# The last normalisation with its scale worked out on transposed statistics, and eight of its tiles prepared by TensorE

## The chip, the cores and the metric

One core of one Trainium2 chip runs the whole kernel in one launch. The metric is the device time of that launch in microseconds (us): 2783.64 as the median of three runs (2782.03 to 2784.01). Below, PE is TensorE, ACT is ScalarE, DVE is VectorE, POOL is GpSimd and SP is the engine that issues most DMAs.

## The reference

Two layers of a streaming encoder work on 288 tokens (256 of a prompt and 32 of a running stream) of width 2048. Layer 0 mixes tokens by a gated MLP, layer 1 by retention; each is followed by a SwiGLU network. After every one of these four parts comes the same step:

```python
def layer_norm(x, g, b):
    mu = jnp.mean(xf, axis=-1, keepdims=True)
    var = jnp.mean(jnp.square(xf - mu), axis=-1, keepdims=True)
    y = (xf - mu) * lax.rsqrt(var + LN_EPS) * g + b
...
x = layer_norm(ALPHA * x + swiglu(x, w_ffn_in[i], w_ffn_out[i]), ln_ffn_g[i], ln_ffn_b[i])
```

The case is about the last of these four normalisations, whose result is the output `yT`.

## The kernel before, in words

All activations lie transposed: 128 features on the partitions and the 288 tokens along the free axis, so that the width of 2048 makes 16 tiles of 128x288, kept in `y`. Weights stream from memory in chunks of 128x1024 fp32. SP loads a chunk into a `raw` buffer (three of them rotate), ACT casts it into a high part (L435) and DVE subtracts that into a low part (L436); PE then makes three products of each 128x128 block (L106 to L108). A chunk is prepared three chunks ahead of its use.

The output product of the last SwiGLU finishes one of the 16 output tiles after another, and `PostNorm.last` is called as each is done. It adds the tile to `y` (L236), subtracts a coarse centre (L284), squares on ACT (L286) and adds tile and square into two running sums (L289, L290). With the last but one tile it also writes an identity and a row of minus ones into a `raw` buffer named `centring` (L254 to L257). After the last tile, `stats` sums over the partitions by matmuls with a constant matrix, which leaves mean `m1` and mean square `m2` of every token, the same on all 128 partitions, in two PSUM banks (L302, L305).

`finish` then normalises. It writes the order of DVE, ACT and POOL out by hand (`manual_schedule` with the three engines of `FINISH`); PE is in hand-written order throughout, and SP takes its DMAs in the order in which they are issued in the code. Its parts:

- The scale `ap` = 1/sqrt(variance) is worked out on full 128x288 tiles: square of the mean and variance (L355, L362), logarithm and exponential on ACT (L363, L364), and one Newton step on DVE (L366 to L368). Variance and scale lie in PSUM; a copy `a` of the scale in SBUF is made for POOL (L370).
- Tiles are handled in pairs (L334, 128x576). Centring subtracts the mean, scaling multiplies by the scale. POOL does both for the pairs 4, 8 and 10, with copies of mean and scale in SBUF. DVE does the pairs 0, 2 and 14, with mean and scale in PSUM. For tiles 6, 7, 12 and 13 PE makes the centred tile in PSUM (L358, L359), and DVE multiplies it by `a` (L341).
- Gain and bias are then applied tile by tile, by ACT for eleven tiles (L351) and by DVE for five (L349), and each finished pair is stored (L352). The first pair stored is 0 and the last store is tile 13; one single tile goes through ACT's queue.

PSUM has eight banks, four in the rotating pool `acc` and four in `aux`.

Of the kernel before, what the change touches and what calls it, by code (L numbers as in the profile page):

```python
# [10 lines left out]
F32 = mybir.dt.float32  # L11
# [3 lines left out]
ALU = mybir.AluOpType  # L15
# [4 lines left out]
P = 128  # L20
# [17 lines left out]
GN_EPS = 1e-6  # L38
CB = 8
RAW = 3  # L40
NBLK = KT * 32 + KT * KT + KT * 96 + 32 * KT + 2 * (KT * 2 * HT + HT * KT)
NSTATE = HEADS * CB
NCH = (NBLK + NSTATE) // CB
# [148 lines left out]
class PostNorm:  # L192
# [38 lines left out]
    def last(self, m, ps, first_part=False):  # L231
        nc, lnp, gi = self.nc, self.lnp, self.gi
        if first_part:
            self.part(m, ps)
        else:
            nc.vector.tensor_tensor(self.y[:, m, :], ps[:, :NT], self.y[:, m, :], ALU.add)  # L236
        if self.n == 0:
            self.s = lnp.tile([P, 2, NT], F32, tag="sums", name=f"sums{gi}")
            nc.gpsimd.memset(self.s, 0.0)
            if self.out is not None:  # L240
                self.core.tables("natural_log_exp_and_others")
            else:
                if gi == 0:
                    self.core.tables("silu_and_others")
                gb = self.cst["ln"][:, gi, :, :].rearrange("p a k -> p k a")
                nc.scalar.copy(self.xh[:, :, NT:NX], gb)
                nc.vector.tensor_tensor(self.xl[:, :, NT:NX], gb, self.xh[:, :, NT:NX].bitcast(F32), ALU.subtract)
            r = self.tmp("cen", F32R)
            nc.scalar.copy(r, self.y[:, m, :])
            self.core.after(2, lambda: self.center(r))  # L250
        self.n += 1
        if self.out is not None and self.n == KT - 1:
            room = self.core.wp.tile([P, CB * P], F32, tag="raw", name="centring", bufs=3)
            self.ident, self.minus = room[:, :P], room[:, P:2 * P]  # L254
            make_identity(nc, self.ident)
            nc.gpsimd.memset(self.minus, 0.0)
            nc.gpsimd.memset(self.minus[:1, :], -1.0)  # L257
            d = self.y[:, KT - 1, :]
            nc.vector.tensor_tensor(d, d, self.c, ALU.subtract)
        if self.c is None:  # L260
            self.wait.append(m)
        else:
            self.sums(m)
        if self.n == (KT if self.out is None else KT - 1):
            self.parts = [[self.tmp(f"s{i}{j}", F32R) for j in range(2)] for i in range(2)]
            for i, (hi, lo) in enumerate(self.parts):
                split(nc, hi, lo, self.s[:, i, :])
        if self.n == KT:
            self.core.after(1 if self.out is not None else 2, lambda: self.stats(m))

    def center(self, r):

        nc = self.nc
        ps = self.core.bank(f"cen{self.gi}")
        nc.tensor.matmul(turned(ps[:, :NT]), self.cst["one_r"], turned(r), start=True, stop=True)
        self.c = self.lnp.tile([P, NT], F32, tag="cen", name=f"cens{self.gi}")
        nc.scalar.mul(self.c, ps[:, :NT], float(KT))
        for q in self.wait:
            self.sums(q)
# [16 lines left out]
    def stats(self, m):  # L296
# [18 lines left out]
        rsqrt(nc, a, v, t)  # L315
        nc.vector.scalar_tensor_tensor(b, m1, -1.0, a, ALU.mult, ALU.mult)

    def finish(self, m1, m2):


        nc, core, a, mean = self.nc, self.core, self.a, self.b
        mm = nc.tensor.matmul
        ap = core.bank("ap")[:, :NT]
        v = core.accum("fin")[:, :NT]
        t, r = self.tmp("t"), self.tmp("r")
        pool = (4, 8, 10)
        copied = (6, 7, 12, 13)
        late = (10, 11, 13, 14, 15)
        row = lambda k: self.y[:, k:k + 2, :]
        off = {k: (core.bank if i == 3 else core.accum)(f"off{k}")[:, :NT] for i, k in enumerate(copied)}  # L330

        def pair(k, op, vec, gp):
            eng, f = (nc.gpsimd, gp) if k in pool else (nc.vector, vec)
            eng.tensor_tensor(row(k), row(k), f.unsqueeze(1).broadcast_to([P, 2, NT]), op)  # L334

        center = lambda k: pair(k, ALU.subtract, m1, mean)

        def scale(k):
            if k in copied:
                for i in (k, k + 1):  # L340
                    nc.vector.tensor_tensor(self.y[:, i, :], off[i], a, ALU.mult)  # L341
            else:
                pair(k, ALU.mult, ap, a)

        def affine(k, n=2, queue=None):
            for i in range(k, k + n):
                d = self.y[:, i, :]
                if i in late:
                    nc.vector.tensor_scalar(d, d, self.gain(i), self.bias(i), ALU.mult, ALU.add)  # L349
                else:  # L350
                    nc.scalar.activation(d, d, AF.Identity, bias=self.bias(i), scale=self.gain(i))  # L351
            (queue or nc.sync).dma_start(self.out[:, k:k + n, :], self.y[:, k:k + n, :])  # L352

        with core.tc.manual_schedule(engines=FINISH):
            nc.scalar.activation(t, m1, AF.Square)  # L355
            nc.scalar.copy(mean, m1)
            for k in copied:
                mm(off[k], self.ident, self.y[:, k, :], start=True, stop=False)  # L358
                mm(off[k], self.minus, mean, start=False, stop=True)  # L359
            for k in pool:  # L360
                center(k)
            nc.vector.scalar_tensor_tensor(v, m2, LN_EPS, t, ALU.add, ALU.subtract)  # L362
            nc.scalar.activation(t, v, AF.Ln)  # L363
            nc.scalar.activation(r, t, AF.Exp, scale=-0.5)  # L364
            center(0)
            nc.vector.scalar_tensor_tensor(ap, v, -0.5, r, ALU.mult, ALU.mult)  # L366
            nc.vector.tensor_tensor(ap, ap, r, ALU.mult)
            nc.vector.scalar_tensor_tensor(ap, ap, 1.5, r, ALU.add, ALU.mult)  # L368
            scale(0)
            nc.scalar.copy(a, ap)  # L370
            for k in pool:
                scale(k)
            center(2)
            affine(0)
            scale(6)
            affine(6)
            scale(2)
            affine(4)
            affine(2)
            center(14)  # L380
            scale(12)
            affine(8)
            scale(14)
            affine(14)
            affine(10)
            affine(12, 1, nc.scalar)
            affine(13, 1)

    def norm(self, k):
        nc, d = self.nc, self.y[:, k:k + 2, :]  # L390
# [521 lines left out]
@with_exitstack  # L912
def hybrid_step(ctx, tc, ins, outs):
    nc = tc.nc
    ctx.enter_context(tc.manual_schedule(engines={PE}))
    core = Core(ctx, tc, ins["wpack"])
    cp = ctx.enter_context(tc.tile_pool(name="cp", bufs=1))
    lnp = ctx.enter_context(tc.tile_pool(name="lnp", bufs=1))
    cp.tile([P, 88], F32, name="shift")
    lnp.tile([P, 32], F32, name="shift_lnp")  # L920
    xh = moving(cp, KT, "xh")
    xl = moving(cp, KT, "xl")
    y = cp.tile([P, KT, NT], F32, name="y")
    cst = {}
    cp.tile([P, 40], F32, name="shift_one")
    cst["one2048"] = cp.tile([P, P], F32, name="one2048")
    nc.gpsimd.memset(cst["one2048"], 1.0 / D)
    cst["ln"] = cp.tile([P, 4, 2, KT], F32, name="lnv")
    cst["one_r"] = cp.tile([P, P], F32R, name="one_r")
    cp.tile([P, 56], F32, name="shift_end")  # L930
    core.tables("gelu_and_others")
    nc.scalar.copy(cst["one_r"], cst["one2048"])
    warm = core.bank("warm")
    for _ in range(11):
        nc.tensor.matmul(warm[:, :P], cst["one2048"], cst["one2048"], start=True, stop=True)

    def load(k):
        if k < KT:
            if k % 2 == 0:
                nc.sync.dma_start(y[:, k:k + 2, :], ins["xT"][:, k:k + 2, :])  # L940
            split(nc, xh[:, k, :NT], xl[:, k, :NT], y[:, k, :])

    with tc.manual_schedule(engines={mybir.EngineType.DVE, mybir.EngineType.Activation}):
        core.prep(0, lambda: load(0))
        for k in range(1, 4):
            load(k)
            core.prep(k)
    x = (xh, xl)
    ln = gmlp(core, cst, x, y, lnp, ins, outs["v"], lambda s: load(s + 4))
    ln = ffn(core, cst, x, y, lnp, 0, ln)  # L950
    ln = retention(core, cst, x, y, lnp, ln, ins, outs["st_p"], outs["st_s"])
    ffn(core, cst, x, y, lnp, 1, ln, outs["yT"])
    core.flush()
    assert len(core.order) == NBLK + NSTATE
    return core.order
# [84 lines left out]
```

## Time and profile before

| what | value |
|---|---|
| median of three runs | 2783.64 us (2782.03 to 2784.01) |
| the profiled execution's own time | 2784.02 us |
| its span in the profile | 2781.9 us |
| PE busy | 2769.4 us (100%) |
| DVE, ACT, POOL busy | 1695.2, 1239.0, 141.4 us (61%, 45%, 5%) |
| moved by DMA | 515.49 MB, mean 185 GB/s |
| last product of the last SwiGLU starts | 2764.83 us after the span's start |
| last store issued | 2777.49 us |
| bytes written by the stores of `yT` | 2.36 MB |

A share of busy time says which engine the whole span belongs to. The stretch that the change touches is the last 17 us; it has to be read from the timeline of that stretch, engine by engine, and from the transfers in it. An instruction's line in a timeline gives its start, its duration, engine, line, operation, output and inputs, and in brackets how long the engine was idle before it and what ended that; "x3" merges three in a row, and the duration is then that of all three.

### The profile page before, as it was taken

The numbers are of one execution on the slowest core, as the hardware profiler recorded it, in microseconds if no ns is written. First come the engines' busy times: TensorE is split into PE (matmuls) and PEld (weight loads), VectorE is DVE, ScalarE is ACT, GpSimd is POOL, SyncE is SP. The second block draws the span as 40 slices with busy tenths as digits, with TensorE's granted clock in tenths as the row PEclk, the third lists the DMA queues.
The fourth block names the chain that finished last, engine by engine and source line by source line (L and its number), as shares of the span: only waits on it lengthen the run. The fifth ranks groups of instructions, "written<-read, shape, count | busy, mean of one in ns | idle before, by whom it ended". The sixth has DMA issues, their size and how long they took to land.

```text
span 2781.9 us, 51416 instructions
## 1 busy us (share of the span) xinstructions
PE 2769.4 (100%) x21574; PEld 2755.9 (99%) x21574; DVE 1695.2 (61%) x2432; ACT 1239.0 (45%) x1641; POOL 141.4 (5%) x241
## 2 busy tenths in 40 slices
PE   9999999999999999999999999999999999999998
PEld 9999999999999999999999999999999999999998
DVE  6688964445444466877765666767864445444465
ACT  5455553333343344554543444445653433333343
POOL 1100000000000000012200111200000000000001
PEclk9999999999999999999999999999999999999999
DMA  8655555555555555567765666755555555555553
GB/s 281 214 186 167 171 169 174 174 174 174 175 173 172 176 177 175 178 199 244 232 197 173 198 216 217 230 193 173 167 175 174 174 172 173 173 174 175 174 174 125
DMA packets 146584, 515.49 MB, mean 185 GB/s; under 512 B 18016, under 2 KB 20336, under 8 KB 146320
## 3 DMA queue, kind: packets, MB, share of 16 engines
q1 hardware_dynamic: 131984, 473.47, 51.4%
q0 software_dynamic: 14224, 38.59, 4.6%
q8 instruction: 168, 2.75, 0.4%
q14 instruction: 64, 0.52, 0.1%
q10 hardware_dynamic: 144, 0.15, 0.0%
HBM read 486.98 MB, written 25.17 MB: 184 GB/s over the span
## 4 chain that ended last, share of the span: by engine, by line
PE 97%; DVE 1%; DMA 1%; issue 0%; POOL 0%; ACT 0%; DVEq 0%; POOLq 0%
PE af_in L107 13%; PE af_in L108 13%; PE af_in L106 13%; PE ab_in L107 7%; PE ab_in L106 7%; PE ab_in L108 7%; PE af_out L108 6%; PE af_out L107 6%; PE af_out L106 6%; PE ab_out L106 2%; PE ab_out L108 2%; PE ab_out L107 2%; PE aa_in L108 2%; PE aa_in L106 2%; PE aa_in L107 2%; PE aa_out L107 1%
## 5 line engine op out<-in xcount | busy, mean ns | idle before, releaser
L436 DVE TENSOR_TENSOR wlo<-raw,whi 128x1024 fp32r<-128x1024 f32 (+1 forms) x892 | 1085.5, 1218 | 865.4 <-ACT whi L435 859.8
L435 ACT CAST whi<-raw 128x1024 fp32r<-128x1024 f32 (+1 forms) x892 | 931.5, 1046 | 1374.4 <-issue 325.9
L107 PE MATMUL af_in<-xl,whi 128*128 128x288 f32 (+1 forms) x2816 | 814.3, 289 | 0.0
L108 PE MATMUL af_in<-xh,wlo 128*128 128x288 f32 (+1 forms) x2816 | 814.1, 289 | 0.0
L106 PE MATMUL af_in<-xh,whi 128*128 128x288 f32 (+1 forms) x2816 | 813.3, 289 | 0.0
L108 PEld LDWEIGHTS af_in<-xh,wlo 128*128 128x128 f32 x2816 | 527.8, 187 | 0.0
L107 PEld LDWEIGHTS af_in<-xl,whi 128*128 128x128 f32 x2816 | 527.8, 187 | 0.0
L106 PEld LDWEIGHTS af_in<-xh,whi 128*128 128x128 f32 x2816 | 527.7, 187 | 0.0
L107 PE MATMUL ab_in<-xl,whi 128*128 128x288 f32 (+1 forms) x1536 | 444.9, 290 | 0.3
L106 PE MATMUL ab_in<-xh,whi 128*128 128x288 f32 (+1 forms) x1536 | 444.3, 289 | 0.0
L108 PE MATMUL ab_in<-xh,wlo 128*128 128x288 f32 (+1 forms) x1536 | 443.7, 289 | 0.0
L107 PE MATMUL af_out<-hl,whi 128*128 128x288 f32 x1408 | 405.9, 288 | 0.0
L106 PE MATMUL af_out<-hh,whi 128*128 128x288 f32 x1408 | 405.9, 288 | 0.0
L108 PE MATMUL af_out<-hh,wlo 128*128 128x288 f32 x1408 | 405.9, 288 | 0.0
L107 PEld LDWEIGHTS ab_in<-xl,whi 128*128 128x128 f32 x1536 | 288.0, 187 | 1.9 <-DVE xl L436 0.7
L106 PEld LDWEIGHTS ab_in<-xh,whi 128*128 128x128 f32 x1536 | 287.9, 187 | 0.9
L108 PEld LDWEIGHTS ab_in<-xh,wlo 128*128 128x128 f32 x1536 | 287.9, 187 | 0.0
L106 PEld LDWEIGHTS af_out<-hh,whi 128*128 128x128 f32 x1408 | 263.8, 187 | 0.0
L107 PEld LDWEIGHTS af_out<-hl,whi 128*128 128x128 f32 x1408 | 263.8, 187 | 0.0
L108 PEld LDWEIGHTS af_out<-hh,wlo 128*128 128x128 f32 x1408 | 263.8, 187 | 0.0
L106 PE MATMUL aa_in<-xh,whi 128*128 128x288 f32 x512 | 148.5, 290 | 0.0
L108 PE MATMUL aa_in<-xh,wlo 128*128 128x288 f32 x512 | 147.8, 289 | 0.2 <-DVE wlo L436 0.2
(246 smaller groups left out, 2906.1 us busy)
## 6 DMA issues: line engine op xcount, KB each, us to landing
raw<-in_wpack_dram SPq DMA_DIRECT2D x887, 512.0 KB, 3.3
v_room<-tv POOLq DMA_DIRECT2D x32, 144.0 KB, 5.0
of<-o_room POOLq DMA_DIRECT2D x32, 144.0 KB, 4.5
vw<-v_room POOLq DMA_DIRECT2D x8, 512.0 KB, 5.7
out_st_s_dram<-sso POOLq DMA_DIRECT2D x16, 256.0 KB, 2.8
o_room<-to POOLq DMA_DIRECT2D x8, 512.0 KB, 3.9
out_st_p_dram<-so POOLq DMA_DIRECT2D x16, 256.0 KB, 5.8
y<-in_xT_dram SPq DMA_DIRECT2D x8, 288.0 KB, 5.4
```

What stands on the lines that cost most here:

```text
L106: mm(ps, hi, xh, start=first, stop=False)
L107: mm(ps, hi, xl, start=False, stop=False)
L108: mm(ps, lo, xh, start=False, stop=last)
L435: nc.scalar.copy(hi, f)
L436: nc.vector.tensor_tensor(lo, f, hi.bitcast(F32), ALU.subtract)
```

## The change

The statistics are transposed in blocks of 32x32, so that one column of nine blocks holds each of the 288 tokens once (32 partitions by 9 columns, repeated on the four quarters of the partitions). Variance, logarithm, exponential and Newton step work on these nine columns; two results are spread back to 288 columns by transposing a broadcast view: `a` = 1/sqrt(variance) and a row of sqrt(variance). `rows` has minus the mean in its first 32 partitions and the square root in the next 32.

For tiles 0 to 7 (`PRE`), PE makes gain * (y - mean) + bias * sqrt(variance) in PSUM: first a product with a diagonal matrix that carries the gain, then one with two rows, gain and bias, against `rows`. DVE multiplies that by `a` (`scaled`), and the pair is stored without further work. The pairs 8, 10 and 12 are centred by POOL and 14 by DVE; POOL scales 8 and 10, DVE scales 12 and 14; ACT applies gain and bias to these eight tiles. `a` and the mean's copy lie in SBUF; the nine-column work lies in SBUF.

The identity, the diagonal matrices and the two rows are made in `factors`, with the last but one tile, in three `raw` buffers instead of one. The two rows come from a new input by two DMAs of SP. The first store is now that of pair 12, then 0, 2, 8, 14, 4, 6 and 10, all on SP's queue.

```diff
@@ last
-            room = self.core.wp.tile([P, CB * P], F32, tag="raw", name="centring", bufs=3)
-            self.ident, self.minus = room[:, :P], room[:, P:2 * P]
...
+            self.factors()
@@
+    def factors(self):
+        ident, diag, gb = (wp.tile([P, CB * P], F32, tag="raw", name=n, bufs=3) for n in ("ident", "diag", "gbrow"))
...
+        make_identity(nc, ident[:, :P])
+        nc.gpsimd.memset(gb, 0.0)
+        for i in range(2):
+            nc.sync.dma_start(gb[32 * i:32 * i + 1, :], self.cst["lnrow"][i:i + 1, :])
+        for k in range(PRE):
+            nc.scalar.mul(self.diag[:, k, :], ident[:, :P], self.gain(k))
@@ finish
+        t1, t2, rows = self.tmp("t1"), self.tmp("t2"), self.tmp("rows")
+        g = self.tmp("g")[:, :4 * NT // 32].rearrange("p (i b) -> p i b", i=4)
+        sq, v, r, u = (g[:, i, :] for i in range(4))
+        one = lambda t: blocks(t)[:, :, 0]
+        spread = lambda t, p=slice(0, P): t[p].unsqueeze(2).broadcast_to([p.stop - p.start, NT // 32, 32])
+        def pair(eng, k, op, f):
             eng.tensor_tensor(row(k), row(k), f.unsqueeze(1).broadcast_to([P, 2, NT]), op)
+        def first(k):
+            pre[k] = (core.bank if k in (4, 5) else core.accum)(f"pre{k}")[:, :NT]
+            mm(pre[k], self.diag[:, k, :], self.y[:, k, :], start=True, stop=False)
+        def second(k):
+            mm(pre[k], self.gb[:64, k, :], rows[:64, :], start=False, stop=True)
+        def scaled(k):
+            nc.vector.tensor_tensor(self.y[:, k, :], pre[k], a, ALU.mult)
...
+            for k in range(6):
+                first(k)
             nc.scalar.copy(mean, m1)
+            nc.vector.transpose(t1, m1)
+            nc.scalar.mul(rows[:32, :], m1[:32, :], -1.0)
+            for k in (8, 10, 12):
+                pair(nc.gpsimd, k, ALU.subtract, mean)
+            nc.vector.tensor_tensor(sq, one(t1), one(t1), ALU.mult)
+            nc.vector.transpose(t2, m2)
+            nc.vector.scalar_tensor_tensor(v, one(t2), LN_EPS, sq, ALU.add, ALU.subtract)
+            nc.scalar.activation(u, v, AF.Ln)
+            nc.scalar.activation(r, u, AF.Exp, scale=-0.5)
+            pair(nc.vector, 14, ALU.subtract, m1)
+            newton(nc, r, r, v, u)
+            nc.vector.tensor_tensor(u, v, r, ALU.mult)
+            nc.vector.transpose(rows[32:64, :], spread(u, slice(32, 64)))
+            nc.vector.transpose(a, spread(r))
+            for k in (8, 10):
+                pair(nc.gpsimd, k, ALU.mult, a)
+            for k in range(6):
+                second(k)
+            pair(nc.vector, 12, ALU.mult, a)
+            affine(12)
+            for k in range(PRE):
+                scaled(k)
+                if k < 2:
+                    first(6 + k)
+                    second(6 + k)
+                if k % 2:
+                    store(k - 1)
+                if k == 3:
+                    pair(nc.vector, 14, ALU.mult, a)
+                    affine(8)
+                    affine(14)
             affine(10)
```

## Rows read from the trace of the kernel before

**Rows 1.** The page's busy times of PE, and its chain of work that ended last, by engine.

```profile
PE 2769.4 (100%) x21574; PEld 2755.9 (99%) x21574; DVE 1695.2 (61%) x2432; ACT 1239.0 (45%) x1641; POOL 141.4 (5%) x241
...
PE 97%; DVE 1%; DMA 1%; issue 0%; POOL 0%; ACT 0%; DVEq 0%; POOLq 0%
```

**Rows 2.** The timeline of the tail, all engines, from the statistics to the last arithmetic.

```profile
2766.52 0.41 ACT L355 ACTIVATE t<-m 128x288 f32<-128x288 f32 x1 [0.37 <-PE m L305]
...
2766.82 0.39 ACT L356 COPY b<-m 128x288 f32<-128x288 f32 x1
2767.05 0.47 DVE L362 SCALAR_TENSOR_TENSOR fin<-m,t 128x288 f32<-128x288 f32 x1 [1.44 <-PE m L305]
2767.30 4.14 POOL L334 TENSOR_TENSOR y<-y,b 128x576 f32<-128x576 f32 x3 [17.00 <-ACT b L356]
...
2771.05 5.81 ACT L351 ACTIVATE y<-y,lnv 128x288 f32<-128x288 f32 x11
2771.30 0.82 DVE L341 TENSOR_TENSOR y<-off,a 128x288 f32<-128x288 f32 x2
2771.40 4.13 POOL L334 TENSOR_TENSOR y<-y,a 128x576 f32<-128x576 f32 x3
2772.04 0.74 DVE L334 TENSOR_TENSOR y<-y,ap 128x576 f32<-128x576 f32 x1
...
2774.87 2.18 DVE L349 TENSOR_SCALAR y<-y,lnv 128x288 f32<-128x288 f32 x5
```

**Rows 3.** The timeline of SP's queue: four of the eight issues of stores, the first three and the last.

```profile
2772.22 0.35 SPq L352 DMA_DIRECT2D out_yT_dram<-y  x1
...
2773.26 0.34 SPq L352 DMA_DIRECT2D out_yT_dram<-y  x1
...
2774.34 0.33 SPq L352 DMA_DIRECT2D out_yT_dram<-y  x1
...
2777.49 0.53 SPq L352 DMA_DIRECT2D out_yT_dram<-y  x1
```

**Rows 4.** Stretches of the tail. The columns after the stretch: its length, busy us (and instructions) of PE, PEld, DVE, ACT and POOL, the granted clock of PE, the busy share of the DMA engines, and GB/s. Then the row of the drains that end the program on SP (shortest, median and longest in ns, first and last start), and the times from issue to landing of the stores.

```profile
2772.50:2773.50 1.00, 0.00 (x0) 0.00 (x0) 1.00 (x3) 1.00 (x3) 1.00 (x2) 1.00 0.43 164
...
2774.00:2774.50 0.50, 0.00 (x0) 0.00 (x0) 0.50 (x2) 0.50 (x2) 0.50 (x2) 0.82 0.81 309
2774.50:2775.00 0.50, 0.00 (x0) 0.00 (x0) 0.46 (x2) 0.50 (x2) 0.50 (x1) 0.50 0.75 281
...
2776.50:2780.00 3.50, 0.00 (x0) 0.00 (x0) 0.56 (x2) 0.36 (x1) 0.00 (x0) 0.50 1.03 373
2780.00:2780.50 0.50, 0.00 (x0) 0.00 (x0) 0.00 (x0) 0.00 (x0) 0.00 (x0) 0.50 0.25 83
...
L1024 SPq DRAIN x3: 7/7/7, 2781.1 to 2781.4; - x3
...
DMA to landing us min/median/max: 2.1/2.2/3.2
```

**Rows 5.** The timeline of DVE and POOL at the two places where a DVE instruction meets a POOL instruction that could share something with it: the first gain and bias on DVE, while POOL's last scaling runs, and the identity's making on POOL, beside the sums of a tile on DVE.

```profile
2774.87 0.82 DVE L349 TENSOR_SCALAR y<-y,lnv 128x288 f32<-128x288 f32 x1
...
2775.62 1.10 DVE L349 TENSOR_SCALAR y<-y,lnv 128x288 f32<-128x288 f32 x3
...
2749.35 0.20 POOL L256 MEMSET centring<- 128x128 f32 x1
...
2749.55 0.46 DVE L284 TENSOR_TENSOR y<-y,cens 128x288 f32<-128x288 f32 x1
2749.59 0.56 POOL masks.py:199 TENSOR_SCALAR_AFFINE_SELECT centring<-centring 128x128 f32<-128x128 f32 x1
...
2750.04 0.46 DVE L289 TENSOR_TENSOR sums<-sums,y 128x288 f32<-128x288 f32 x1
```

**Rows 6.** Groups of instructions by line, engine, operation and shape over the whole span (busy us, mean ns of one, idle before and its releasers): the nearest to the new small ones, a transposition of 128x288 out of PSUM, a POOL memset, and ACT on tiles of 32 and of 128 columns. Then two of the three-column ones from the timeline, one behind the other.

```profile
L189 DVE SCALAR_TENSOR_TENSOR gn<-gn 128x3 f32<-128x3 f32 x24 | 3.9, 164 | 0.8
...
L685 DVE STREAM_TRANSPOSE tv<-ab_in 128x288 f32<-128x288 f32 x28 | 13.2, 471 | 12.4 <-PE ab_in L108 12.4
...
L239 POOL MEMSET sums<- 128x576 f32 x4 | 2.3, 578 | 416.9 <-DVE s L436 416.9
...
L246 ACT CAST xh<-lnv 128x32 fp32r<-128x32 f32 x3 | 0.7, 223 | 0.0
...
L932 ACT CAST one_r<-one 128x128 fp32r<-128x128 f32 x1 | 0.3, 298 | 0.0
...
1612.27 0.16 DVE L188 TENSOR_TENSOR gn<-gn 128x3 f32<-128x3 f32 x1
1612.47 0.16 DVE L189 SCALAR_TENSOR_TENSOR gn<-gn 128x3 f32<-128x3 f32 x1
```

**Rows 7.** The timeline of PE in the tail: two products of the centring by PE, one behind the other without a wait.

```profile
2767.92 0.65 PE L358 MATMUL off<-y,centring 128*128 128x288 f32 x2
2768.41 0.65 PE L359 MATMUL off<-b,centring 128*128 128x288 f32 x2
```

**Rows 8.** The timeline of ACT and DVE around the last chunk of weights: the end of the last chunk's split on DVE, and ACT's idle time before the square of the last but one tile.

```profile
2752.91 1.05 ACT L435 CAST whi<-raw 128x1024 fp32r<-128x1024 f32 x1 [1.48 <-issue]
...
2754.00 1.23 DVE L436 TENSOR_TENSOR wlo<-raw,whi 128x1024 fp32r<-128x1024 f32 x1 [1.31 <-ACT whi L435]
...
2757.78 0.45 ACT L286 ACTIVATE sq<-y 128x288 f32<-128x288 f32 x1 [3.82 <-DVE y L284]
```

More of the change, by code (lines that the diff above doesn't have):

```diff
@@ L40 @@
 RAW = 3
+PRE = 8
 NBLK = KT * 32 + KT * KT + KT * 96 + 32 * KT + 2 * (KT * 2 * HT + HT * KT)
@@ L252, in last @@
         if self.out is not None and self.n == KT - 1:
-            room = self.core.wp.tile([P, CB * P], F32, tag="raw", name="centring", bufs=3)
-            self.ident, self.minus = room[:, :P], room[:, P:2 * P]
-            make_identity(nc, self.ident)
-            nc.gpsimd.memset(self.minus, 0.0)
-            nc.gpsimd.memset(self.minus[:1, :], -1.0)
+            self.factors()
             d = self.y[:, KT - 1, :]
@@ L316, in stats @@
         nc.vector.scalar_tensor_tensor(b, m1, -1.0, a, ALU.mult, ALU.mult)
+    def factors(self):
+        nc, wp = self.nc, self.core.wp
+        ident, diag, gb = (wp.tile([P, CB * P], F32, tag="raw", name=n, bufs=3) for n in ("ident", "diag", "gbrow"))
+        self.diag = diag.rearrange("p (k c) -> p k c", c=P)
+        self.gb = gb.rearrange("p (k c) -> p k c", c=P)
+        make_identity(nc, ident[:, :P])
[4 more added lines that the diff above has]
+            nc.scalar.mul(self.diag[:, k, :], ident[:, :P], self.gain(k))
     def finish(self, m1, m2):
@@ L322, in finish @@
         mm = nc.tensor.matmul
[L323 to L328, printed above, removed]
+        t1, t2, rows = self.tmp("t1"), self.tmp("t2"), self.tmp("rows")
+        g = self.tmp("g")[:, :4 * NT // 32].rearrange("p (i b) -> p i b", i=4)
+        sq, v, r, u = (g[:, i, :] for i in range(4))
+        blocks = lambda t: t.rearrange("p (b s) -> p b s", s=32)
@@ L329, in finish @@
+        one = lambda t: blocks(t)[:, :, 0]
+        spread = lambda t, p=slice(0, P): t[p].unsqueeze(2).broadcast_to([p.stop - p.start, NT // 32, 32])
         row = lambda k: self.y[:, k:k + 2, :]
-        off = {k: (core.bank if i == 3 else core.accum)(f"off{k}")[:, :NT] for i, k in enumerate(copied)}
-        def pair(k, op, vec, gp):
-            eng, f = (nc.gpsimd, gp) if k in pool else (nc.vector, vec)
+        pre = {}
+        def pair(eng, k, op, f):
             eng.tensor_tensor(row(k), row(k), f.unsqueeze(1).broadcast_to([P, 2, NT]), op)
-        center = lambda k: pair(k, ALU.subtract, m1, mean)
@@ L338, in scale @@
[L338 to L346, printed above, removed]
-                d = self.y[:, i, :]
[L348 to L352, printed above, removed]
+        def first(k):
+            pre[k] = (core.bank if k in (4, 5) else core.accum)(f"pre{k}")[:, :NT]
+            mm(pre[k], self.diag[:, k, :], self.y[:, k, :], start=True, stop=False)
@@ new lines, in second, with store, affine @@
+        def second(k):
+            mm(pre[k], self.gb[:64, k, :], rows[:64, :], start=False, stop=True)
+        def scaled(k):
+            nc.vector.tensor_tensor(self.y[:, k, :], pre[k], a, ALU.mult)
+        def store(k, n=2, queue=None):
+            (queue or nc.sync).dma_start(self.out[:, k:k + n, :], self.y[:, k:k + n, :])
+        def affine(k):
+            for i in (k, k + 1):
+                d = self.y[:, i, :]
+                nc.scalar.activation(d, d, AF.Identity, bias=self.bias(i), scale=self.gain(i))
+            store(k)
@@ L354, in finish @@
         with core.tc.manual_schedule(engines=FINISH):
-            nc.scalar.activation(t, m1, AF.Square)
+            for k in range(6):
+                first(k)
             nc.scalar.copy(mean, m1)
[L357 to L384, printed above, removed]
+            nc.vector.transpose(t1, m1)
[4 more added lines that the diff above has]
+            nc.vector.transpose(t2, m2)
@@ L385, in finish @@
+            for k in range(6):
[13 more added lines that the diff above has]
+                    affine(14)
             affine(10)
-            affine(12, 1, nc.scalar)
@@ L387, in finish @@
-            affine(13, 1)
     def norm(self, k):
@@ L927, in hybrid_step @@
     nc.gpsimd.memset(cst["one2048"], 1.0 / D)
+    cst["lnrow"] = ins["lnrow"]
     cst["ln"] = cp.tile([P, 4, 2, KT], F32, name="lnv")
@@ L1005 @@
     data["lnv"] = ca(np.array(lnv).transpose(2, 0, 1, 3))
+    data["lnrow"] = ca(np.stack([a[f"ln_ffn_{t}"][1] for t in "gb"])[:, :PRE * P])
     data["a_gb"] = ca(np.broadcast_to(np.stack([a["a_ln_g"][0], a["a_ln_b"][0]])[None], (P, 2, D)))
```

## The prediction

> **What bounds the kernel now.** I read the page first: PE is busy for all of the span and is 97% of the chain that ended last [rows 1], so nothing before the last product can matter unless it holds PE up. The change touches only what follows that product, so the next view was the timeline of the last 17 us, engine by engine. There the reader is to see the statistics ready at 2766.5, three centrings on POOL from 2767.30, and arithmetic on DVE until 2777.05 (2774.87 + 2.18) [rows 2]. A chain of waits that ends in DVE suggests that DVE's work sets the end. The stretches of the tail say otherwise: from 2776.5 to 2780.0 the DMA engines are busy without a break (share 1.03) at 373 GB/s, three microseconds after the arithmetic is over [rows 4]. The end is the transfer of the output.
>
> That gives a formula for the end. The first store is issued at 2772.22 [rows 3]. The stretch from 2772.5 to 2773.5 carries 164 KB [rows 4], which at 373 GB/s is 0.44 us, so the bytes began at 2773.06, 0.84 after the issue. All 2.36 MB of the stores take 6.33 us at that rate. Without a gap they would end at 2779.39. The stretch from 2780.0 carries 83 x 0.5 = 41 KB, or 0.11 us, so they ended at 2780.11: there were 0.72 us of gaps, early on, when stores came singly at 2772.22, 2773.26 and 2774.34 [rows 3]. From the last byte to the span's end pass 1.79 us, with SP's drains at 2781.1 [rows 4]; nothing in the change shortens that. So the span is: issue of the first store + 0.84 + 6.33 + gaps + 1.79. What the arithmetic's end is worth depends on these two quantities alone: how early the first store goes, and whether later ones come fast enough (one per 0.79 us, an eighth of 6.33) to leave no gap.
>
> **The change part by part.**
>
> *Preparation.* ACT's eight products of the identity with a gain are 8 x 0.30 = 2.4 us at the row for 128x128 [rows 6]. The diagonal's buffer comes free when DVE has split the last chunk but one; ACT is done with its last cast at 2753.96 and idle for 3.82 us before the square at 2757.78 [rows 8]. They fit, so nothing; if they went ahead of that cast, the last chunk would be split 2.4 us later than 2755.23, and PE needs it only some 3 us before its last product at 2764.83, so still nothing. POOL's memset of 1024 columns is 1024/576 x 0.58 = 1.03 us [rows 6], after 2755.23. The two small DMAs on SP pass no store, which come 15 us later, and if they land as the stores do, within 3.2 us [rows 4], the rows lie ready by 2760.
>
> *Mean and POOL.* The square of the mean on full tiles leaves ACT, so the mean's copy starts at 2766.52 instead of 2766.82 and takes 0.39; POOL follows it by 0.09 as before (2767.21 to 2767.30), at 2767.00. Three centrings take 4.14 [rows 2], 1.38 each: they end at 2768.38, 2769.76 and 2771.14. Pair 12, the first to be stored, is the third of them.
>
> *The scale.* A transposition of 288 columns is 0.47, a nine-column instruction on DVE is 0.20 from one start to the next (1612.27 to 1612.47, three columns), one on ACT about 0.22 (32 columns) [rows 6]. Unhindered: first transposition from 2766.52, or from 2766.91 if it must wait for ACT's copy out of the same bank, to 2767.4; square of the mean to 2767.6; second transposition to 2768.05; variance to 2768.25; logarithm and exponential to 2768.8; DVE centres pair 14 meanwhile, 0.74, to 2769.0; Newton's three and the square root 4 x 0.20 to 2769.8; two transpositions, about 0.43 each, to 2770.7. The scale would then be ready before POOL is.
>
> But it may be held. The kernel before gives its DVE instructions beside POOL one operand in PSUM each. The new square, variance, Newton steps and root have both operands in SBUF, and so have the scalings of pairs 12 and 14. The trace has two places that bear on this [rows 5]. The first gain and bias on DVE meets POOL's last scaling (2771.40 + 4.13 = 2775.53, [rows 2]): it takes 0.82 instead of the 0.37 that three later ones take each (1.10 in all), and ends at 2775.69. So it ran from 2775.3 on: held by POOL's instruction until about 0.2 us before the end of that row. It has one tensor operand, though, so it need not speak for two. The other place does: the sum of tile and centre, with both inputs in SBUF, runs from 2749.55 to 2750.01, and POOL's select, which reads SBUF, starts at 2749.59 and takes 0.56 where a memset of the same size takes 0.20, ending 0.14 after DVE's. That is what holding would look like, but I have no row of an undisturbed select, and the next DVE sum at 2750.04 is not lengthened. The bounds of the hold are nothing (as at 2750.04) and all POOL has queued. I take one POOL instruction for each DVE instruction that meets one, because the first row shows a wait that ends with the running instruction.
>
> The Trainium skill, "SBUF — State Buffer", section "Who interferes with whom", states a rule against this change: a DVE instruction with two SBUF inputs contends with a GpSimd instruction that reads SBUF, and the later of the two waits for the whole of the other. The trace agrees for the 0.82 us instruction, which the same section puts down to another mode of DVE; for two SBUF inputs no row here settles it. By the rule the sum is the one below, without it that of the first rival.
>
> Held, the order is: square behind centring 1, variance behind centring 2 (logarithm, exponential and pair 14 fit before centring 3 ends), Newton behind centring 3, until 2771.14 - 0.2 = 2770.94. Then POOL has nothing left until the scale exists: 4 x 0.20 and two transpositions, 0.80 + 0.87, to 2772.6.
>
> *From the scale to the first store.* Pair 12 on DVE 0.74 to 2773.35; ACT's two tiles 2 x 0.53 (5.81 / 11, [rows 2]) to 2774.43; SP's issue 0.07 later, at 2774.5. The stores of 0 and 2, ready sooner, stand behind it on SP's queue. Since DVE starts pair 12 before POOL's scaling gets the scale across engines, I let DVE go first; if POOL goes first, 1.4 us more.
>
> *The feed behind it.* From 2774.5 on a store is needed every 0.79. Tiles 0 to 3 cost DVE 0.37 each [rows 2] and are done at 2774.85; PE's six second products at 0.49 each (2767.92 to 2768.41, [rows 7]) from 2772.2 are ahead of them. POOL scales 8 by 2774.75, ACT finishes it at 2775.8, needed 2776.9. Pair 14 waits on DVE behind POOL's scaling of 10 at worst, until 2776.1; ACT ends it at 2777.9, needed 2777.65: a gap of 0.3 at most. Tiles 4 to 7 are done by 2778.3 and pair 10 by 2779.1, needed by 2778.4 to 2780.0. So the gaps shrink from 0.72 to between 0 and 0.3; DVE's five gains and biases (2.18) and the full-size Newton step are gone, but that saves nothing beyond those gaps, since the transfer is what ends.
>
> **Sum.** Span 2774.5 + 0.84 + 6.33 + 1.79 = 2783.46 against 2781.9: +1.6 us. The profiled execution took 2784.02, that is 2.12 around its span, so it would take 2785.6; it lay 0.38 above the median of the runs. Median 2783.64 + 1.6 = 2785.2.
>
> **The rivals.**
>
> *A. DVE is not held: not slower.* The scale is ready at 2770.7 and pair 12 waits for POOL's third centring, 2771.14. Then 0.74, 1.06 and 0.07: first store at 2773.0, span 2773.0 + 8.96 = 2781.96, +0.1. Median 2783.7. For it speaks the unlengthened sum at 2750.04 [rows 5]. It decides if the square and the variance take 0.2 each beside POOL. Even here nothing is won: the first store is 0.8 later than before, and that eats the 0.72 of gaps.
>
> *B. The forecast, 2785.2;* its own range is 2784.3 to 2786.7, from DVE slipping its last nine-column steps ahead of centring 3 (-0.6) to POOL's scaling going ahead of pair 12 (+1.4).
>
> *C. POOL keeps its turn: more than that slower.* If a waiting DVE instruction doesn't get in between two queued POOL instructions, the square runs only at 2770.94. Then 0.2 + 0.47 + 0.2 + 0.55 + 0.8 + 0.87 to 2774.0, 1.4 after the forecast: +3.0, median 2786.6. If POOL's scalings of 8 and 10 go ahead of pair 12 too, 2 x 1.38 more: +5.8, 2789.4. Against it: the held instruction of [rows 5] began before POOL's row had ended, so there is an opening.
>
> *D. PE's clock.* It falls from full to half at about 2774.3, 3.3 us after PE's last product [rows 4]. If it fell while PE waits for the scale (2769.8 to 2772.2), products would take 0.98 each and tile 7 would come at 2781 instead of 2778.3: store 6 at 2781.1, nearly 2 us after it is needed, 2787. PE resumes within 2.4 us, so this is unlikely.
>
> *E. The change doesn't do what it says:* one of the new rows or diagonals is late and PE waits at its first product. Their covers are 9 us long, so hardly.
>
> **How the numbers follow.** Chances: B 0.58, A 0.24, C 0.12 (a third of it the dear form), D 0.04, E 0.02. The range takes in A less the scatter of the runs (1 us either way, 2782.03 to 2784.01) and the cheap C: 2782.8 to 2787.2. What a measurement of this kernel can tell from no change is 0.2%, 5.6 us. Only the dear C exceeds it: slower 0.04, faster 0.01, no change 0.95.
>
> **What would show it.** The first row of `yT` on SP's queue: at 2774.5 (A 2773.0, C 2775.9 or later). The nine-column rows on DVE: some lasting about a microsecond while POOL centres (B), all 0.2 (A). The DMA share: 1.0 from about 2775.5 until the last byte at 2781.7, no gap over 0.3. If the bytes end sooner than 6.3 us after they begin, or the span's end doesn't follow them by 1.8, the formula is wrong; a span under 2781 would refute the whole argument.

## The result, and the profile after

The changed kernel takes 2788.80 us (median of 14 runs, 2786.12 to 2790.95) against 2783.46 for the kernel before in the same measurement (14 runs): ratio 1.0018, interval 1.0011 to 1.0025, that is 5.3 us slower. The forecast was 2785.2 with a range to 2787.2: the direction was right, the size a third of what came, and the time lies 1.6 us outside the range. The interval lies wholly above 1, so the loss is told from no change, though it is under the 0.2% (5.6 us) that the prediction gave as the least that can be told.

Executions begin the tail at slightly different times (the add of the last tile starts at 2765.15 before and at 2765.75 after). So below I compare the *tail*: from the start of that add to the end of the span. It is 2781.9 - 2765.15 = 16.75 us before and 2787.9 - 2765.75 = 22.15 after, +5.4, as much as the times differ. Each tail is that of one profiled execution. The two adds, before and after:

```profile
2765.15 0.46 DVE L236 TENSOR_TENSOR y<-af_out,y 128x288 f32<-128x288 f32 x1 [5.47 <-PE af_out L108]
```
```profile
2765.75 0.46 DVE L237 TENSOR_TENSOR y<-af_out,y 128x288 f32<-128x288 f32 x1 [5.48 <-PE af_out L109]
```

The tail's timeline after, DVE and POOL (start, duration, engine, line, operation, output and inputs). The first four lines are from the preparation, 17 us earlier.

```profile
2749.80 0.20 POOL masks.py:197 MEMSET ident<- 128x128 f32 x1 [783.44 <-DMA raw<-in_wpack_dram]
2750.08 0.29 POOL masks.py:199 TENSOR_SCALAR_AFFINE_SELECT ident<-ident 128x128 f32<-128x128 f32 x1
...
2750.14 0.54 DVE L281 TENSOR_TENSOR y<-y,cens 128x288 f32<-128x288 f32 x1
2750.71 0.46 DVE L286 TENSOR_TENSOR sums<-sums,y 128x288 f32<-128x288 f32 x1
...
2767.53 4.13 POOL L343 TENSOR_TENSOR y<-y,b 128x576 f32<-128x576 f32 x3 [13.16 <-ACT b L367]
...
2768.00 0.97 DVE L372 TENSOR_TENSOR g<-t 128x9 f32<-128x9 f32 x1
...
2769.40 0.93 DVE L374 SCALAR_TENSOR_TENSOR g<-t,g 128x9 f32<-128x9 f32 x1
...
2770.92 0.77 DVE L188 SCALAR_TENSOR_TENSOR g<-g 128x9 f32<-128x9 f32 x1
2771.72 0.17 DVE L189 TENSOR_TENSOR g<-g 128x9 f32<-128x9 f32 x1
...
2772.83 0.48 DVE L381 STREAM_TRANSPOSE a<-g 128x288 f32<-128x288 f32 x1
```

While POOL's three centrings run (2767.53 to 2771.66), three nine-column instructions of DVE last 0.77 to 0.97; as soon as POOL is done, the next lasts 0.17. The scale is ready at 2773.31, 7.56 us after the last tile's add.

PE and the end of DVE in the same timeline:

```profile
2767.82 2.59 PE L347 MATMUL pre<-y,diag 128*128 128x288 f32 x10
2773.01 5.29 PE L350 MATMUL pre<-rows,gbrow 64*128 64x288 f32 x12 [2.60 <-issue]
2778.23 1.32 PE L347 MATMUL pre<-y,diag 128*128 128x288 f32 x2
2779.48 1.32 PE L350 MATMUL pre<-rows,gbrow 64*128 64x288 f32 x2
2780.74 1.33 PE L347 MATMUL pre<-y,diag 128*128 128x288 f32 x2
2781.99 1.33 PE L350 MATMUL pre<-rows,gbrow 64*128 64x288 f32 x2
...
2783.36 0.46 DVE L353 TENSOR_TENSOR y<-pre,a 128x288 f32<-128x288 f32 x1 [2.06 <-PE pre L350]
```

Three rows of the same kernel by stretch (columns as in [rows 4]; the clock is the third number from the right):

```profile
2773.00:2774.00 1.00, 0.99 (x4) 0.83 (x5) 0.90 (x2) 0.00 (x0) 0.55 (x1) 0.92 0.00 0
2774.00:2775.00 1.00, 1.00 (x3) 0.70 (x3) 0.95 (x3) 0.79 (x2) 1.00 (x1) 0.50 0.09 16
2781.20:2784.60 3.40, 2.12 (x4) 0.54 (x3) 0.56 (x2) 0.00 (x0) 0.00 (x0) 0.50 0.00 0
```

PE has no work for 2.60 us while the scale is made. It resumes at 2773.01, and at 2773.84 (0.84 of the first stretch at full clock, the rest at half, makes 0.92) the granted clock falls from 2.4 to 1.2 GHz. The six second products then take 5.29 us, and the four of tiles 6 and 7, which stand behind them in PE's order, take 1.25 each. They don't wait for a free PSUM bank, as the first expectation below has it: tiles 0 and 1, whose banks they take over, are scaled by 2774.95, and their first product starts at 2778.23. DVE's last scaling starts at 2783.36, behind 2.06 us of waiting for PE. From 2781.2 to 2784.6 nothing is transferred at all: the stores have run dry.

SP's queue, its first two stores and its last two, and then the scalings and the gains and biases that the first two wait for:

```profile
2774.98 0.38 SPq L356 DMA_DIRECT2D out_yT_dram<-y  x1
...
2775.41 0.42 SPq L356 DMA_DIRECT2D out_yT_dram<-y  x1
...
2783.84 0.81 SPq L356 DMA_DIRECT2D out_yT_dram<-y  x2
```
```profile
2774.09 0.86 DVE L353 TENSOR_TENSOR y<-pre,a 128x288 f32<-128x288 f32 x2
2774.21 2.40 ACT L361 ACTIVATE y<-y,lnv 128x288 f32<-128x288 f32 x4 [3.39 <-DVE y L343]
```

By the formula of the prediction, the first store's issue + 0.84 + 6.33 + 1.79 without gaps, the span would end at 2783.94. It ends at 2787.9: 4.0 us of gaps, 3.4 of them the empty stretch above. The first store is not that of pair 12, as I had it, but that of pair 0: it goes 0.03 after tiles 0 and 1 are scaled, and the second when ACT's two tiles of pair 12 are done. So SP does not take its DMAs in the order of the code, as the description of the kernel before has it; the orders written out by hand are those of PE, DVE, ACT and POOL.

### The profile page after: what moved, and what is told of

Its sections match the earlier page's. It is cut to its first block, busy times and chain, and to the rows that moved or that the text cites. A ratio compares the mean times of both kernels' runs of the same rounds, so it can differ in the third digit from the quotient of the medians.

```text
span 2787.9 us, 51451 instructions
## 1 busy us (share of the span) xinstructions
PE 2779.4 (100%) x21590; PEld 2761.4 (99%) x21590; DVE 1696.2 (61%) x2434; ACT 1240.3 (44%) x1645; POOL 141.0 (5%) x239
## 4 chain that ended last, share of the span: by engine, by line
PE 99%; DMA 0%; DVE 0%; POOL 0%; issue 0%; ACT 0%; POOLq 0%
PE af_in L108 13%; PE af_in L109 13%; PE af_in L107 13%; PE ab_in L108 7%; PE ab_in L107 7%; PE ab_in L109 7%; PE af_out L108 6%; PE af_out L109 6%; PE af_out L107 6%; PE aa_in L109 2%; PE aa_in L107 2%; PE aa_in L108 2%; PE ab_out L109 2%; PE ab_out L108 2%; PE ab_out L107 2%; PE aa_out L108 1%
## 5 line engine op out<-in xcount | busy, mean ns | idle before, releaser
L108 PE MATMUL aa_in<-xl,whi 128*128 128x288 f32 x512 | 147.8, 289 | 0.0
```

Source lines behind the costliest of these rows:

```text
L108: mm(ps, hi, xl, start=False, stop=False)
```

## The experiments

**PE kept busy.** Theory: the loss beyond the forecast is PE's clock. Five more products of tile 5 fill PE's wait.

```diff
-            for k in range(6):
+            for k in range(5):
                 first(k)
+            pre[5] = core.bank("pre5")[:, :NT]
+            for i in range(6):
+                mm(pre[5], self.diag[:, 5, :], self.y[:, 5, :], start=True, stop=i < 5)
```

> PE makes the first product of tile 5 five times more than needed (the repeats are overwritten), 5 x 0.49 = 2.45 us, so that it is busy while it waits for the scale; the result is the same. Theory 1 (after its 2.6 us of idling the granted clock falls to half at 2773.8, and the products behind it, above all the four of tiles 6 and 7 which must wait for a free bank, take double time and set the end): the clock stays at 1.00 through the second products, they come every 0.49, the last add of DVE comes near 2778.5 instead of 2783.4, the stores have no gap over 1 us, and the time falls by 3.5 to 4.5 us against the changed kernel, to about 2784.8 (ratio to before 1.0003 to 1.0007). Theory 2 (the second products are slow for another reason: 64 rows, or DVE): no change, 2788.8. Theory 3 (the held nine-column steps alone set the loss): no change, 2788.8. The nine-column steps of 0.77 to 0.97 us stay as they are.

Measured: 2785.68 us against 2783.57 before, ratio 1.0005 (0.9995 to 1.0014); the profiled tail is 2782.2 - 2763.32 = 18.9 us instead of 22.15. The timelines of DVE, PE and SP, and a stretch with the products of tiles 6 and 7:

```profile
2765.57 0.97 DVE L375 TENSOR_TENSOR g<-t 128x9 f32<-128x9 f32 x1
...
2770.59 3.15 PE L350 MATMUL pre<-rows,gbrow 64*128 64x288 f32 x12 [0.18 <-issue]
...
2772.95 0.38 SPq L356 DMA_DIRECT2D out_yT_dram<-y  x1
...
2774.26 0.37 SPq L356 DMA_DIRECT2D out_yT_dram<-y  x1
...
2775.70 0.75 PE L350 MATMUL pre<-rows,gbrow 64*128 64x288 f32 x2
...
2776.49 0.46 DVE L353 TENSOR_TENSOR y<-pre,a 128x288 f32<-128x288 f32 x1 [0.40 <-PE pre L350]
```
```profile
2775.00:2776.00 1.00, 1.00 (x4) 0.59 (x4) 1.00 (x3) 0.97 (x2) 0.00 (x0) 1.00 0.90 339
```

PE idles 0.18 us, the second products take 3.15 instead of 5.29, and DVE's last scaling comes 13.2 us after the last tile's add instead of 17.6. DVE is held as before (0.97). 3.3 us of the 5.4 thus go with the clock. That is a net figure, since SP's order isn't the same here: the first store is that of pair 12, 9.63 us after the add instead of 9.23. The gaps, by the formula, fall from 4.0 to 0.3. What is left, 2.1 in the tail, is what the forecast had put at 1.6.

**POOL silent, and POOL only writing.** Theory: DVE's nine-column steps are held because both their inputs lie in SBUF while POOL reads SBUF. Rival: they are slow by themselves (their first inputs lie 32 columns apart), or any POOL instruction holds them. The first run has only the removed lines, the second also the added ones.

```diff
-            for k in (8, 10, 12):
-                pair(nc.gpsimd, k, ALU.subtract, mean)
+            for _ in range(12):
+                nc.gpsimd.memset(self.sq, 0.0)
```

> POOL doesn't centre the pairs 8, 10 and 12 (their centring is left out); nothing else is changed. Theory 1 (a DVE instruction with both inputs in SBUF is held by a POOL instruction that reads SBUF): the nine-column square, variance and first Newton step take about 0.2 us each instead of 0.97, 0.93 and 0.77; the scale is ready 1.9 to 2.2 us earlier after the last tile's add (5.5 us behind it instead of 7.6); PE idles under 1 us and its clock stays up, so that the time falls by 5 to 6 us, to about 2783. Rival (the small instructions are slow by themselves, by their columns that lie 32 apart): they take as long as before, and the time stays within 0.5 us of 2788.8.

> Instead of centring the pairs 8, 10 and 12 (left out), POOL writes zeros twelve times over a tile that is no longer needed, some 4 us of instructions that read nothing. If what holds DVE is the reading of SBUF by POOL, the nine-column steps take 0.2 us each as without POOL. If any POOL instruction holds it, they stay near a memset's length (0.3 us more each).

Measured, one run each: 2784.38 and 2784.33 us, beside 2783.57 for the kernel before. The nine-column square and variance, and PE's second products, first without POOL; then the square and variance beside POOL's memsets:

```profile
2768.40 0.18 DVE L370 TENSOR_TENSOR g<-t 128x9 f32<-128x9 f32 x1
...
2769.00 0.17 DVE L372 SCALAR_TENSOR_TENSOR g<-t,g 128x9 f32<-128x9 f32 x1
...
2771.27 3.14 PE L350 MATMUL pre<-rows,gbrow 64*128 64x288 f32 x12 [0.45 <-issue]
```
```profile
2768.46 4.69 POOL L371 MEMSET sq<- 128x288 f32 x12 [13.20 <-PE m L302]
...
2768.90 0.17 DVE L372 TENSOR_TENSOR g<-t 128x9 f32<-128x9 f32 x1
...
2769.50 0.17 DVE L374 SCALAR_TENSOR_TENSOR g<-t,g 128x9 f32<-128x9 f32 x1
```

0.18 instead of 0.97 without POOL, and 0.17 in the midst of POOL instructions that read nothing. Both rivals fall. PE then waits 0.45 us instead of 2.60 and its second products take 3.14: the hold makes the wait in which the clock is lost, so it costs twice. Both kernels leave out the centring of three pairs, and both tails are shorter than before the change: 2782.4 - 2766.15 = 16.3 and 2782.4 - 2766.65 = 15.8 us. The first time lies 1.4 us above what was expected, which one run can't tell.

**The nine columns in PSUM.** The same question with POOL's centrings kept: square, variance and the intermediate of the Newton step go to free columns of the PSUM bank of the mean square (`nine`, columns 288 to 323), ACT makes the square, and no nine-column step of DVE reads SBUF twice.

```diff
-        sq, v, r, u = (g[:, i, :] for i in range(4))
+        r, u = (g[:, i, :] for i in range(2))
+        n = nine.rearrange("p (i b) -> p i b", i=4)
+        sq, v, w = (n[:, i, :] for i in range(3))
...
+            nc.scalar.activation(sq, one(t1), AF.Square)
-            nc.vector.tensor_tensor(sq, one(t1), one(t1), ALU.mult)
...
-            newton(nc, r, r, v, u)
+            nc.vector.scalar_tensor_tensor(w, v, -0.5, r, ALU.mult, ALU.mult)
+            nc.vector.tensor_tensor(w, w, r, ALU.mult)
+            nc.vector.scalar_tensor_tensor(r, w, 1.5, r, ALU.add, ALU.mult)
```

> The nine-column square, variance and Newton intermediate lie in free columns of the PSUM bank of the mean square, and ACT makes the square, so that no nine-column instruction of DVE but has at most one input in SBUF; POOL centres as in the changed kernel; the result is the same. Theory 1 (held by two SBUF inputs): each nine-column instruction takes about 0.2 us although POOL runs, the scale is ready about 5.7 us after the last tile's add instead of 7.6, PE idles about 1 us, its clock stays up; the time falls by 4 to 6 us, to 2783 to 2784.8. Rival (any DVE instruction of this kind is delayed beside POOL, or small ones are slow): the steps stay at 0.8 to 1.0 us and the time at 2788.8.

Measured: 2783.71 us against 2783.57, ratio 0.9999 (0.9989 to 1.0009); tail 2780.8 - 2763.40 = 17.4 us. The timelines of POOL, DVE, PE and SP:

```profile
2765.19 4.13 POOL L345 TENSOR_TENSOR y<-y,b 128x576 f32<-128x576 f32 x3 [13.17 <-ACT b L369]
...
2766.45 0.18 DVE L376 SCALAR_TENSOR_TENSOR m<-t,m 128x9 f32<-128x9 f32 x1
...
2767.20 0.17 DVE L380 SCALAR_TENSOR_TENSOR m<-m,g 128x9 f32<-128x9 f32 x1
...
2768.51 0.48 DVE L385 STREAM_TRANSPOSE a<-g 128x288 f32<-128x288 f32 x1
2769.35 1.95 DVE L345 TENSOR_TENSOR y<-y,a 128x576 f32<-128x576 f32 x1 [0.36 <-POOL y L345]
...
2768.69 3.15 PE L352 MATMUL pre<-rows,gbrow 64*128 64x288 f32 x12 [0.63 <-issue]
...
2772.06 0.85 SPq L358 DMA_DIRECT2D out_yT_dram<-y  x2
```

With POOL at work no step is held (the variance ends with POOL's first centring and shows little, but the Newton steps run in the midst of the second); the scale is ready 5.59 us after the last tile's add instead of 7.56, PE idles 0.63 us and keeps its clock through the second products. No loss against the kernel before can be measured any more. The tail is still 0.65 longer than before, and the fifth line shows one hold that is left: the scaling of pair 12, still with two inputs in SBUF, meets POOL's first scaling and takes 1.95 instead of 0.75.

**Six tiles by PE.** Is it the clock as such, or the chain of tiles 6 and 7 at that clock?

```diff
             pair(nc.vector, 14, ALU.subtract, m1)
+            pair(nc.vector, 6, ALU.subtract, m1)
...
-            for k in range(PRE):
+            for k in range(6):
                 scaled(k)
-                if k < 2:
-                    first(6 + k)
-                    second(6 + k)
...
+                    pair(nc.vector, 6, ALU.mult, a)
...
+                    affine(6)
```

> Tiles 6 and 7 are not made by PE but as a DVE pair like 14 (centred beside the logarithm, scaled by DVE, gain and bias by ACT); the six others as in the changed kernel; PE idles 2.6 us as there. Theory 1 (the clock falls, and what ends the kernel is the chain of the four products of tiles 6 and 7 at half clock, each 1.25 us, behind the sixth second product): the clock still falls, the six second products still take over 5 us, but nothing follows them; ACT's ten gains and biases end about 2780.5 in the changed kernel's time, and the time falls by 2.5 to 3.5 us, to about 2785.8. Rival (any product at half clock is enough to lose it all): the time falls by under 1 us.

Measured: 2786.29 us against 2783.54, ratio 1.0011 (1.0002 to 1.0020); tail 2784.0 - 2765.09 = 18.9. The timelines of PE, DVE and SP (its first store), and one stretch:

```profile
2772.39 4.68 PE L350 MATMUL pre<-rows,gbrow 64*128 64x288 f32 x12 [2.65 <-issue]
...
2773.47 1.22 DVE L353 TENSOR_TENSOR y<-pre,a 128x288 f32<-128x288 f32 x3
...
2774.32 0.38 SPq L356 DMA_DIRECT2D out_yT_dram<-y  x1
```
```profile
2773.00:2774.00 1.00, 1.00 (x6) 0.71 (x5) 1.00 (x3) 0.41 (x1) 1.00 (x1) 0.92 0.00 0
```

The clock falls here too (PE idles 2.65 us and the six second products take 4.68), but no tile follows them on PE, and the tail is as short as with PE kept busy. The same order of work at full clock was not run. But by the formula the half clock can have cost at most 0.7 us in this trace: the first store, 9.23 us after the add as in the changed kernel, doesn't wait for PE (DVE scales tiles 0 to 2 right behind pair 12), and 2774.32 + 8.96 = 2783.28, 0.7 before the span's end. The rest of the clock's cost belongs to the two tiles that stand last on PE at that clock.

**A shorter wait of PE.** The first experiment with one repeat and with three instead of five (`range(2)` and `range(4)`).

> The changed kernel with one repeat of tile 5's first product instead of five, so that PE idles about 2.1 us before the second products instead of 2.6 (0.18 with five); the result is the same. Theory 1 says nothing of where between 0.18 and 2.6 the clock begins to fall: if it falls here too, the tail from the last tile's add is near 22 us, as in the changed kernel; if it stays, near 18.9, as with five.

> The same with three repeats, idle about 1.15 us. If the clock stays, the tail is near 18.9 us; if it falls, near 22. A tail between the two, with a clock that is full for all second products, would speak against theory 1.

Measured, one run each: 2791.00 and 2786.27 us, beside 2782.33 for the kernel before. The timelines of PE, with one repeat and then with three, and one stretch of each:

```profile
2770.45 1.13 PE L369 MATMUL pre<-y,diag 128*128 128x288 f32 x4
2773.69 5.86 PE L350 MATMUL pre<-rows,gbrow 64*128 64x288 f32 x12 [2.11 <-issue]
```
```profile
2773.22 3.15 PE L350 MATMUL pre<-rows,gbrow 64*128 64x288 f32 x12 [1.16 <-issue]
```
```profile
2773.00:2774.00 1.00, 0.31 (x1) 0.29 (x2) 0.95 (x2) 0.00 (x0) 0.00 (x0) 0.97 0.00 0
```
```profile
2777.00:2778.00 1.00, 1.00 (x4) 0.57 (x4) 1.00 (x3) 0.34 (x1) 0.01 (x1) 1.00 1.03 389
```

With 2.11 us of idling the clock falls and the tail is 2789.2 - 2766.44 = 22.8 us; with 1.16 it stays and the tail is 2784.5 - 2765.95 = 18.6. No tail lies between the two. Their first stores go 9.80 and 9.64 us after the add (2776.24 and 2775.59), so by the formula the difference is gaps: 4.0 us with one repeat and none with three.

**Stores earlier.** A try for something better than both. On top of the nine columns in PSUM, tiles 0 to 3 are scaled first, and the pairs 12 and 14 take the scale from a copy in PSUM; then also the store of pair 8 on ACT's queue.

```diff
+            nc.scalar.copy(m1, a)
-            pair(nc.vector, 12, ALU.mult, a)
-            affine(12)
...
                 if k == 3:
-                    pair(nc.vector, 14, ALU.mult, a)
+                    pair(nc.vector, 12, ALU.mult, m1)
                     affine(8)
-                    affine(14)
+                    affine(12)
+                if k == 5:
+                    pair(nc.vector, 14, ALU.mult, m1)
             affine(10)
+            affine(14)
```

> On top of the nine columns in PSUM: tiles 0 to 3 are scaled right behind the scale, before the pairs 12 and 14, whose scaling takes the scale from a copy in PSUM that ACT makes over the mean, so that no pair of DVE has two inputs in SBUF; the result is the same. Theory 1 (the end is the first store's issue + 8.96 us + gaps): the first store goes 1.5 us earlier than with the nine columns in PSUM alone, that of pair 8 stands ahead of that of 2 in SP's queue and makes a gap of about 0.7; the span is 0.6 to 1.2 us shorter than there (ratio to before about 0.9996). POOL's two scalings take 1.4 us each instead of 3.3 for both. Rival (the arithmetic's end sets it): the last gain and bias ends as late as before, no gain.

> The same, with the store of pair 8 on ACT's queue, so that the stores of 0 and 2 follow one another on SP's. Theory 1: the gap of 0.7 goes, the span is another 0.3 to 0.7 us shorter (ratio to before about 0.9994). Rival: ACT's issue of 0.4 us delays its last gain and bias, and the last store ends later; no gain over the one before.

Measured: 2784.05 us, ratio 1.0001 (0.9992 to 1.0010), and 2783.81, ratio 0.9999 (0.9991 to 1.0008). Tails 2782.1 - 2765.49 = 16.6 and 2781.9 - 2765.34 = 16.6, against 16.75 before. The timeline of SP and DVE in the second form:

```profile
2772.36 0.38 SPq L358 DMA_DIRECT2D out_yT_dram<-y  x1
...
2776.54 0.46 DVE L355 TENSOR_TENSOR y<-pre,a 128x288 f32<-128x288 f32 x1 [0.82 <-PE pre L352]
...
2777.02 1.30 SPq L358 DMA_DIRECT2D out_yT_dram<-y  x3
```

The mechanism works: the first store goes 7.0 us after the last tile's add instead of 8.7 with the nine columns in PSUM alone, and POOL's scalings take 2.8 together instead of 3.3. But it is no earlier than in the kernel before (2772.22 - 2765.15 = 7.1), and tile 7, again last on PE, is scaled at 2776.54 and lets SP's last three stores go only at 2777.02. No gain over the kernel before can be measured, and the second form is no better than the first beyond what the runs scatter. Against the nine columns in PSUM alone the tails are 0.8 shorter, as expected of the first form, but the times don't show it.

## Why the prediction failed, point by point

*What bounds the tail* held. The end follows the transfers: issue of the first store + 8.96 + gaps gives 2783.94 + 4.0 after, 2781.02 for the nine columns in PSUM (first store 2772.06; the span is 2780.8, so no gap). A span under 2781 after the change didn't come. The term of the sum that failed is the gaps: put at 0 to 0.3, and 4.0 by the formula.

*The hold* was right in kind and size. Square behind centring 1, variance behind centring 2, first Newton step behind centring 3, one DVE instruction per POOL instruction: all three rows are there. The scale was forecast 7.45 us after the last tile's add and came at 7.56. The undecided evidence of [rows 5] has its counterpart in the preparation above, which fits the hold: here the select started first and took 0.29, and it was DVE's sum with two SBUF inputs that grew, to 0.54; before, DVE started first, DVE took 0.46 and the select 0.56. The rule cited from the Trainium skill ("SBUF — State Buffer", "Who interferes with whom") agrees with all runs, also in its clause that a GpSimd instruction which only writes doesn't contend (0.17 beside the memsets). Rivals A and C fall: A's steps of 0.2 came only without POOL's reading or with PSUM, and DVE got in between two queued POOL instructions. The dear form of C, 2789.4, lies nearest the measured time, but by chance: its mechanism isn't in the trace.

*The sum of that part* was 1.6 and measured 2.1 in the tail with PE kept busy (the times differ by 2.1 as well). Half of the rest is the first store, 9.63 us after the add where 9.35 was forecast (2774.5 - 2765.15); the other half is 0.3 us of gaps, which the sum left out and the text allowed. They don't come from pair 14, though: it was held by POOL's scaling, as forecast (1.82 us in that trace), but the gap lies between the first store and the second, 2772.95 and 2774.26. The 2.1 is within the forecast's own range.

*The step that failed* is the dismissal of rival D, "PE resumes within 2.4 us, so this is unlikely", with a chance of 0.04, and with it the second products at 0.49 in "the feed behind it". The wait of 2.4 us was right (2.60). From one fall 3.3 us after the last product [rows 4] I read that PE is safe if it resumes sooner. It isn't: after the change PE had been at work again for 0.8 us when the clock fell. The price given for D, 2787, was low too: tile 7's scaling was put at 2781, 15.9 us after the last tile's add, and came 17.6 after it. Part of that is a slip in the sum (ten products at 0.98 from 2772.2 end at 2782.0, not 2781), and part is that the last four took 1.25 each and not 0.98 (also at full clock, with PE kept busy, they come every 0.68 and not every 0.49: 2775.02 to 2775.70).

*SP's order* was wrong in the first place of the queue (0 before 12). It moved the first store by no more than 0.4: pair 12, which went second, would have gone at 2775.4.

## What to carry to other kernels

A small DVE instruction is not cheap beside GpSimd: with both its inputs in SBUF it waited here for the GpSimd instruction that ran and read SBUF, 0.97 us for nine columns that take 0.17 by themselves; one operand in PSUM removed that. Work that TensorE does in two halves with a wait between them is to be priced at both clocks, and repeats of a product that are overwritten were a cheap guard for the wait (2788.80 to 2785.68 us). Where the output's transfer ends the kernel, count from the first store and look for the moment when the stores run dry; here that was the tile left for last on TensorE.

## What had not been expected

The granted clock does not fall at a fixed time after PE's last product. From the end of the products before the idle stretch to the fall it was 3.3 us in the kernel before, 3.4 after the change (2770.41 to 2773.84, PE at work again for 0.8), 2.4 with one repeat (2771.58 to 2773.94) and 4.1 with six tiles by PE (2769.75 to 2773.84, PE at work again for 1.5). An idle stretch of 1.16 us had no fall in the products behind it, yet with the nine columns in PSUM the clock fell 1.6 us after the last product of all. What sets the moment stays open here.
